# Head sums of squares by PE transposes and DVE row sums, and the mixers' large POOL operations on DVE and ACT

## The chip, the core and the metric

One core of one Trainium2 chip runs the whole program as one launch. The metric is device microseconds of one execution, median of three runs. The engines are called by the profile's names: PE (TensorE; its weight loads are the row PEld), DVE (VectorE), ACT (ScalarE), POOL (GpSimd) and SP (which here only issues DMAs). Each works through its own instructions in a fixed order, and waits on the others by semaphores.

## What is computed

One encoder layer over 1024 new prompt rows and 32 sample rows (T = 1056 token columns). The change touches the mixers between the two feed-forward parts:

```python
h = rms_norm(x, mix_norm)
sq, sk, sv, hq, hf, hi, hg = split(h @ w_in, ...)
sq = rms_norm(heads(sq, 8), sb_q_gain)             # per head of 64
sk = rms_norm(heads(sk, 8), sb_k_gain)
sb_o = rms_norm(sb_mix(sq, sk, sv), sb_out_gain)   # stick-breaking attention, per head of 64
f = lb + (1.0 - lb) * sigmoid(hf)
k_in = (1.0 - lb) * sigmoid(-hf)
q_h = silu(hq)
o_h, S_new = hgrn2_scan(q_h, k_in, hi, log(f), S0) # 4 heads of 128
o_h = rms_norm(o_h, hg_out_gain) * silu(hg)        # per head of 128
x = x + concat([sb_o, o_h]) @ w_out
```

All is float32. Each per-head `rms_norm` needs one sum of squares per token and head.

## The kernel before

Features lie on the 128 partitions and tokens on the free axis, in three groups of 384, 384 and 288 tokens (`GROUPS`). The program has a feed-forward part (to about 740 us), the mixers (about 740 to 1480 us) and a second feed-forward part. In the mixers `project_stream` multiplies 28 slabs of `w_in` (tile `pp`, L840, each product as three matmuls of split operands), and `mix_stream` those of `w_out` (`ps`, L1447). Between these, `merge` lays the steps of the attention streams (`z`, `pt`, `av`), the sample streams and the scans (`hg_stream`); a scheduler sets each engine's final order from that and from priorities. So the filler matmuls `pp` stand between the small steps of the streams, and the order does not change at run time.

Two things are touched.

**Sums of squares.** `token_factors` gets the squares `sq` (128 features by up to 384 tokens; two heads of 64 or one of 128 on the partitions). Each block of 128 tokens is a matmul (L222, tile `pmc`) with `sq` as the weights and a two-column or one-column matrix of 1/64 or 1/128 (`g.hd`, `g.od`) as the moving side. DVE reads the few sums from PSUM (L226 with a factor for the token, or L229 with the epsilon); POOL adds the epsilon (L227), raises to -1/2 (L230) and multiplies by the token's factor (L232). `spread` then widens the factors on ACT (L242, `wide`), PE transposes them (L249, `pb`), and DVE multiplies them in (L926, L933, L1054, L1415). It is called 52 times: 24 for q and k, 16 for the attention's output, 12 for the scans' output, in 140 blocks of 128 tokens and 4 of 32.

**Large elementwise work on POOL.** In `hg_jobs`: (1 - lb) and lb on `hk` and `hf` (L1276, L1278), and the products with a sigmoid for `hq` and `hg` (L1283). In `hg_stream`: seven levels of a doubling scheme per head. A level has PE products `pl` (L1347); then, on the 1024 prompt tokens, `hk` times `hf` on POOL (L1358), and `hq` times `hf` (L1360), a predicated copy of `pl` into `att` (L1362) and an update of `hf` (L1363) on DVE. The next level's `pl` reads `hk` and `hq`. At the end stands the gate (L1417). In `sb_jobs`: the low part of the split values `V` (L974; the high part is a cast on DVE, L973).

The PSUM tiles `pmc`, `pb`, `pl` and others share three buffers (tag `px`).

Of the kernel before, what the change touches and what calls it, by code (L numbers as in the profile page):

```python
# [24 lines left out]
TG = 384  # L25
# [34 lines left out]
def more_consts(g, pool, w):  # L60
# [152 lines left out]
def token_factors(g, f, psp, sq, w, means, behind_, tokens=None):  # L213


    nc = g.nc
    nb, rows, nh = -(-w // P), min(w, P), means.shape[1]
    mc = psp.tile([P, 512], F32, name="pmc", tag="px", bufs=3)
    v = f[0:rows, 0:nb, 0:nh]
    with behind(g, behind_):  # L220
        for b in range(nb):
            nc.tensor.matmul(mc[0:rows, b * nh:(b + 1) * nh], sq[:, b * P:b * P + rows], means, start=True, stop=True)  # L222
    src = mc[0:rows, 0:nb * nh].rearrange("p (b h) -> p b h", h=nh)
    wide = lambda t: t[:, :, None].broadcast_to([rows, nb, nh])
    if tokens is not None:
        nc.vector.tensor_tensor(out=v, in0=src, in1=wide(g.r2[0:rows, tokens]), op=ALU.mult)  # L226
        nc.gpsimd.tensor_scalar(out=v, in0=v, scalar1=1.0, scalar2=EPS, op0=ALU.mult, op1=ALU.add)  # L227
    else:
        nc.vector.tensor_scalar(out=v, in0=src, scalar1=EPS, scalar2=None, op0=ALU.add)  # L229
    nc.gpsimd.tensor_tensor(out=v, in0=v, in1=g.mh[0:rows, :, None].broadcast_to([rows, nb, nh]), op=ALU.pow)  # L230
    if tokens is not None:
        nc.gpsimd.tensor_tensor(out=v, in0=v, in1=wide(g.rc[0:rows, tokens]), op=ALU.mult)  # L232
# [633 lines left out]
def sb_jobs(g, m, pool, psp, gi, outs):  # L866
# [30 lines left out]
    def qk(nm, gain):  # L897
        def evacuate(n, ps):
# [15 lines left out]
            def factors():  # L914
                with g.tc.high_priority():
                    token_factors(g, f[:, b0:b0 + 3], psp, sq, TG, g.hd, g.filler, slice(b0, b0 + 3))
                    if nm == "qn":
                        nb = min(3, 8 - b0)
                        nc.gpsimd.tensor_scalar(out=t.minus[:, b0:b0 + nb], in0=f[:, b0:b0 + nb], scalar1=-1.0,
                                                scalar2=0.0, op0=ALU.mult, op1=ALU.add)  # L920
                        return sample_q if n == NG - 1 else None
                return normed
# [44 lines left out]
    def rows(n):  # L967
# [5 lines left out]
        nc.vector.tensor_copy(hi, src)  # L973
        nc.gpsimd.tensor_tensor(out=lo, in0=src, in1=hi, op=ALU.subtract)  # L974
# [66 lines left out]
def sb_out_norm(g, pool, psp, o, w, out):  # L1041
# [3 lines left out]
    def factors(c):  # L1045
# [4 lines left out]
        token_factors(g, f[c], psp, sq, cw, g.hd, g.filler)  # L1050
# [198 lines left out]
def hg_jobs(g, m, pool, psp, hh):  # L1249
# [5 lines left out]
    def evac(nm):  # L1255
        def evacuate(n, ps):
# [12 lines left out]
            if nm == "hf":  # L1269

                if n == 0:
# [4 lines left out]
                nc.gpsimd.tensor_scalar(out=kd, in0=kd, scalar1=g.olb[:, hh:hh + 1], scalar2=0.0,  # L1276
                                        op0=ALU.mult, op1=ALU.add)
                nc.gpsimd.tensor_scalar(out=xd, in0=xd, scalar1=g.olb[:, hh:hh + 1], scalar2=g.lb[:, hh:hh + 1],  # L1278
                                        op0=ALU.mult, op1=ALU.add)
            else:  # L1280
                a = pool.tile([P, TG], F32, name="sp", tag="sq", bufs=2)[:, 0:gw(n)]
                nc.scalar.activation(a, xd, AF.Sigmoid)
                nc.gpsimd.tensor_tensor(out=xd, in0=xd, in1=a, op=ALU.mult)  # L1283
# [25 lines left out]
def hg_stream(g, m, pool, psp, hh, state, outs, out):  # L1309
# [28 lines left out]
    while m_ < P:  # L1338

        for b, (b0, nch, L) in enumerate(blocks):  # L1340
# [16 lines left out]
            eng = nc.gpsimd if b == 0 else nc.vector  # L1357
            eng.tensor_tensor(out=kv[:, :, 0, :], in0=kv[:, :, 0, :], in1=tr.broadcast_to([P, nb2, m_]),  # L1358
# [45 lines left out]
    def factors(n):  # L1404
# [6 lines left out]
        token_factors(g, fo[n], psp, sq, TG, g.od, g.filler)  # L1411

    def normed(n):
# [3 lines left out]
        nc.gpsimd.tensor_tensor(out=o[:, gs(n)], in0=o[:, gs(n)], in1=sg[:, gs(n)], op=ALU.mult)  # L1417
# [460 lines left out]
```

## Time and profile before

| | us |
|---|---|
| median of 3 runs (2212.99 to 2214.30) | 2213.72 |
| the profiled execution | 2215.67 |
| its span, first to last instruction | 2214.0 |
| PE busy | 2152.4 (97%) |
| DVE, ACT, POOL busy | 1437.6, 928.3, 721.8 |
| PE, DVE, POOL busy in 740 to 1480 us | 720.0, 465.9, 233.5 |
| mean granted TensorE clock | 0.988 |

Busy time of PE includes the modelled ends of pipelined matmuls, so it says where PE had work, not that it ran at its peak. A float32 product is two records (two loads, two matmuls); a transpose of a float32 block, and a product of split operands, is one. "Idle before" in a row is time in which that engine had nothing to run, with what ended it.

### The profile page before, as it was taken

The page shows a single profiled execution, that of the slowest core. Times are in us where ns is not written, and L with a number is a line of the kernel's source. Part 1 is how long each engine was busy: PE and PEld are TensorE (multiplying, and loading weights), DVE is VectorE, ACT ScalarE, POOL GpSimd, SP SyncE. Part 2 cuts the span into 40 slices and gives each one's busy share as a digit, 9 for nine tenths or more (in the row PEclk, how much of TensorE's full clock was granted, in tenths as well). Part 3 has the DMA queues.
Part 4 walks back from the last instruction along what each step waited for, and adds up shares of the span by engine and source line. Part 5 has one row for each costly group of instructions (what it writes and reads, how often), then busy time and mean ns, then how long its engine had stood idle before and what let it go on. Part 6 is the DMA issues. An engine that isn't in the chain of part 4 may idle for free.

```text
span 2214.0 us, 41837 instructions
## 1 busy us (share of the span) xinstructions
PE 2152.4 (97%) x16475; PEld 2102.7 (95%) x16475; DVE 1437.6 (65%) x2461; ACT 928.3 (42%) x1812; POOL 721.8 (33%) x957
## 2 busy tenths in 40 slices
PE   8999999999999999999999999998999999999998
PEld 7999999999999999999999998898999999999998
DVE  5876666654668457567567578449766666645675
ACT  6423333323447444454544555236322333334443
POOL 1455544440004322333333333122555543420000
PEclk9999999999999998999999999999999999999999
DMA  8575454448534210120120122383676455467343
GB/s 239 177 214 170 140 183 153 151 130 295 180 128 153 91 55 20 43 69 20 43 69 20 46 80 79 122 251 124 210 221 193 139 179 162 143 218 243 126 150 122
DMA packets 328806, 307.30 MB, mean 139 GB/s; under 512 B 26593, under 2 KB 284897, under 8 KB 328609
## 3 DMA queue, kind: packets, MB, share of 16 engines
q1 hardware_dynamic: 259456, 264.75, 37.0%
q10 hardware_dynamic: 68672, 38.25, 6.0%
q8 instruction: 129, 2.11, 0.4%
q0 software_dynamic: 480, 1.62, 0.2%
q14 instruction: 69, 0.56, 0.1%
HBM read 208.46 MB, written 96.11 MB: 138 GB/s over the span
## 4 chain that ended last, share of the span: by engine, by line
PE 52%; DVE 5%; DMA 4%; POOL 2%; issue 2%; ACT 1%; SPq 0%; DVEq 0%; ACTq 0%; POOLq 0%
PE bk L389 15%; PE pp L840 14%; PE bk L704 10%; PE pl L1347 2%; PE ps L1447 2%; PE av L1116 1%; PE pt L1097 1%; PE pmc L222 1%; PE z L1152 1%; PE z L1151 1%; DVE t L1010 1%; PE ps L1468 1%; PE pb L249 1%; DMA xp<-xd 1%; DMA gt<-pd 0%
## 5 line engine op out<-in xcount | busy, mean ns | idle before, releaser
L704 PE MATMUL bk<-tl,wh 128*128 128x256 f32 x1232 | 351.3, 285 | 4.6 <-DVE tl L662 4.5
L704 PE MATMUL bk<-th,wl 128*128 128x256 f32 x1232 | 350.1, 285 | 0.4 <-DVE wl L651 0.4
L704 PE MATMUL bk<-th,wh 128*128 128x256 f32 x1232 | 348.8, 284 | 0.9 <-ACT th L661 0.8
L840 PE MATMUL pp<-xs_a,wh 128*128 128x384 f32 (+1 forms) x1008 | 263.8, 343 | 0.0
L704 PEld LDWEIGHTS bk<-tl,wh 128*128 128x128 f32 x1232 | 232.7, 189 | 6.4 <-DVE tl L662 6.4
L704 PEld LDWEIGHTS bk<-th,wl 128*128 128x128 f32 x1232 | 232.5, 189 | 0.9 <-DVE wl L651 0.7
L704 PEld LDWEIGHTS bk<-th,wh 128*128 128x128 f32 x1232 | 231.6, 189 | 1.6 <-ACT th L661 1.3
L544 POOL TENSOR_TENSOR gt<-gt,b 128x256 f32<-128x256 f32 x88 | 73.8, 839 | 328.0 <-ACT gt L543 319.4
L840 PEld LDWEIGHTS pp<-xs_a,wh 128*128 128x128 f32 x1008 | 171.0, 191 | 6.0 <-issue 4.1
L651 DVE SCALAR_TENSOR_TENSOR wl<-oraw,wh 128x1024 fp32r<-128x1024 f32 x84 | 97.9, 1166 | 104.9 <-ACT wh L650 104.8
L840 PE MATMUL pp<-xs_a,wl 128*128 128x384 f32 (+1 forms) x504 | 165.5, 328 | 0.0
L650 ACT ACTIVATE wh<-oraw 128x1024 fp32r<-128x1024 f32 x84 | 83.7, 997 | 147.3 <-PE bk L704 127.7
L389 PE MATMUL bk<-ops_a,wh 128*128 128x272 f32 (+1 forms) x704 | 132.9, 289 | 2.0 <-ACT e L370 2.0
L163 ACT ACTIVATE wh<-wraw 128x512 fp32r<-128x512 f32 (+2 forms) x122 | 89.2, 747 | 106.5 <-PE pp L840 37.2
L543 ACT ACTIVATE gt<-gt 128x256 f32<-128x256 f32 x88 | 37.3, 424 | 224.2 <-DVE gt L510 224.1
L164 DVE TENSOR_TENSOR wl<-wraw,wh 128x512 fp32r<-128x512 f32 (+2 forms) x122 | 110.3, 918 | 29.9 <-ACT wh L163 29.1
L548 POOL TENSOR_TENSOR gt<-gt,b 128x256 f32<-128x256 f32 x88 | 89.1, 1013 | 80.3 <-DVE b L510 80.3
L389 PEld LDWEIGHTS bk<-ops_a,wh 128*128 128x128 f32 x704 | 111.2, 192 | 2.6 <-ACT e L370 2.5
L389 PE MATMUL bk<-ops_a,wl 128*128 128x272 f32 (+1 forms) x352 | 101.1, 288 | 2.6 <-DVE wl L164 2.6
L1514 POOL TENSOR_TENSOR rstd<-rstd,nsq 128x512 f32<-128x512 f32 (+1 forms) x28 | 33.8, 1233 | 205.2 <-ACT nsq L1513 205.2
L1008 ACT ACTIVATE t<-z,minus 128x128 f32<-128x128 f32 (+2 forms) x96 | 55.6, 580 | 98.8 <-PE z L1154 75.4
L840 PEld LDWEIGHTS pp<-xs_a,wl 128*128 128x128 f32 x504 | 96.3, 191 | 0.0
(467 smaller groups left out, 6980.0 us busy)
## 6 DMA issues: line engine op xcount, KB each, us to landing
wraw<-in_ffn_w_in_dram SPq DMA_DIRECT2D x58, 512.0 KB, 4.3
oraw<-in_ffn_w_out_dram SPq DMA_DIRECT2D x94, 256.0 KB, 4.6
sd<-osum SPq DMA_DIRECT2D x44, 512.0 KB, 3.1
gd<-gt SPq DMA_DIRECT2D x42, 528.0 KB, 5.0
braw<-in_ffn_w_in_dram ACTq DMA_DIRECT2D x42, 512.0 KB, 4.3
oraw<-sd SPq DMA_DIRECT2D x40, 512.0 KB, 3.7
oraw<-in_ffn_w_out_dram SPq DMA_DIRECT2D x30, 512.0 KB, 3.4
wraw<-in_w_in_dram SPq DMA_DIRECT2D x28, 512.0 KB, 3.7
```

What stands on the lines that cost most here:

```text
L163: nc.scalar.activation(hi, src, AF.Copy)
L164: return nc.vector.tensor_tensor(out=lo, in0=src, in1=hi, op=ALU.subtract)
L389: mm = g.nc.tensor.matmul(ps, wt[x][:, kk, :], xt[y][:, kk, :], start=(first and kk == 0 and n == 0), stop=(kk == HK - 1 and n == len(PASS ...
L544: nc.gpsimd.tensor_tensor(out=gt[:, 1, cc], in0=gt[:, 1, cc], in1=s["b2"], op=ALU.mult)
L548: last = nc.gpsimd.tensor_tensor(out=gt[:, 0, cc], in0=gt[:, 0, cc], in1=s["b1"], op=ALU.mult)
L650: nc.scalar.activation(h, r, AF.Copy, scale=0.5)
L651: nc.vector.scalar_tensor_tensor(out=l, in0=r, scalar=0.5, in1=h, op0=ALU.mult, op1=ALU.subtract)
L704: nc.tensor.matmul(ps, wt[a][:, d * P:(d + 1) * P], xt[b][:, cols(c)], start=(k == 0 and n == 0), stop=(k == FH - 1 and n == len(PASSES) - 1))
L840: g.filler = nc.tensor.matmul(ps[:, 0:gw(n)], wt[a][:, k, :], xs(b, k)[:, gs(n)], start=(k == 0 and j == 0), stop=(k == KC - 1 and j == le ...
L1008: nc.scalar.activation(a, z, AF.Sigmoid, scale=minus)
L1347: nc.tensor.matmul(pl[0:L, c, 0:hl].rearrange("p (b m) -> p b m", m=m_), k[:, cs(b, c)], qr, start=True, stop=True)
L1447: nc.tensor.matmul(ps[:, 0:w], wt[a][:, k, :], xs(b, c)[:, gs(n)], start=(k == 0 and i == 0), stop=(k == 5 and i == len(PASSES) - 1))
```

## The change

`token_factors` now transposes each block of `sq` (tokens to partitions) and lets DVE sum the rows from PSUM with one TENSOR_REDUCE over 64 or 128 elements. The token's factor and the mean with its epsilon go to POOL: one more small POOL operation in each of the 52 calls. `hd` and `od` go. The gate, the products with sigmoids, `hf`'s affine step and the levels' `hk` move from POOL to DVE, `hk`'s scaling to ACT, `V`'s high part from DVE to ACT and its low part from POOL to DVE.

```diff
@@ -61,13 +62,6 @@
     nc = g.nc
     g.identr = pool.tile([P, P], F32R, name="identr")
     nc.vector.tensor_copy(g.identr, g.ident)
-
-    g.hd = pool.tile([P, 2], F32, name="hd")
-    nc.gpsimd.memset(g.hd, 0.0)
-    nc.gpsimd.memset(g.hd[0:64, 0:1], 1.0 / 64)
-    nc.gpsimd.memset(g.hd[64:128, 1:2], 1.0 / 64)
-    g.od = pool.tile([P, 1], F32, name="od")
-    nc.gpsimd.memset(g.od, 1.0 / P)
     g.zero = pool.tile([P, 1], F32, name="zero")
     nc.gpsimd.memset(g.zero, 0.0)
 
@@ -210,23 +204,22 @@
 EXP_LN, SIGMOID = "natural_log_exp_and_others", "sigmoid_and_others"
 
 
-def token_factors(g, f, psp, sq, w, means, behind_, tokens=None):
-
-
-    nc = g.nc
-    nb, rows, nh = -(-w // P), min(w, P), means.shape[1]
-    mc = psp.tile([P, 512], F32, name="pmc", tag="px", bufs=3)
+def token_factors(g, f, psp, sq, w, behind_, tokens=None):
+
+
+    nc = g.nc
+    nb, rows, nh = -(-w // P), min(w, P), f.shape[2]
+    mc = psp.tile([P, 3, P], F32, name="pmc", tag="px", bufs=3)
     v = f[0:rows, 0:nb, 0:nh]
     with behind(g, behind_):
         for b in range(nb):
-            nc.tensor.matmul(mc[0:rows, b * nh:(b + 1) * nh], sq[:, b * P:b * P + rows], means, start=True, stop=True)
-    src = mc[0:rows, 0:nb * nh].rearrange("p (b h) -> p b h", h=nh)
+            nc.tensor.transpose(mc[0:rows, b, :], sq[:, b * P:b * P + rows], g.ident)
+    nc.vector.tensor_reduce(out=v.rearrange("p b h -> p (b h)"),
+                            in_=mc[0:rows, 0:nb, :].rearrange("p b (h d) -> p (b h) d", h=nh), axis=AX.X, op=ALU.add)
     wide = lambda t: t[:, :, None].broadcast_to([rows, nb, nh])
     if tokens is not None:
-        nc.vector.tensor_tensor(out=v, in0=src, in1=wide(g.r2[0:rows, tokens]), op=ALU.mult)
-        nc.gpsimd.tensor_scalar(out=v, in0=v, scalar1=1.0, scalar2=EPS, op0=ALU.mult, op1=ALU.add)
-    else:
-        nc.vector.tensor_scalar(out=v, in0=src, scalar1=EPS, scalar2=None, op0=ALU.add)
+        nc.gpsimd.tensor_tensor(out=v, in0=v, in1=wide(g.r2[0:rows, tokens]), op=ALU.mult)
+    nc.gpsimd.tensor_scalar(out=v, in0=v, scalar1=nh / P, scalar2=EPS, op0=ALU.mult, op1=ALU.add)
     nc.gpsimd.tensor_tensor(out=v, in0=v, in1=g.mh[0:rows, :, None].broadcast_to([rows, nb, nh]), op=ALU.pow)
     if tokens is not None:
         nc.gpsimd.tensor_tensor(out=v, in0=v, in1=wide(g.rc[0:rows, tokens]), op=ALU.mult)
@@ -913,7 +906,7 @@
 
             def factors():
                 with g.tc.high_priority():
-                    token_factors(g, f[:, b0:b0 + 3], psp, sq, TG, g.hd, g.filler, slice(b0, b0 + 3))
+                    token_factors(g, f[:, b0:b0 + 3], psp, sq, TG, g.filler, slice(b0, b0 + 3))
                     if nm == "qn":
                         nb = min(3, 8 - b0)
                         nc.gpsimd.tensor_scalar(out=t.minus[:, b0:b0 + nb], in0=f[:, b0:b0 + nb], scalar1=-1.0,
@@ -970,8 +963,8 @@
         o, b0, nb = natural(lambda c, e: t.vT[:, GROUPS[n][0] + c:GROUPS[n][0] + c + e], n, outs["v_p"], True)
         src = o[:, 0:nb, :].rearrange("p b (h d) -> p b h d", h=2)
         hi, lo = t.V[:, b0:b0 + nb, :, 0:64], t.V[:, b0:b0 + nb, :, 64:128]
-        nc.vector.tensor_copy(hi, src)
-        nc.gpsimd.tensor_tensor(out=lo, in0=src, in1=hi, op=ALU.subtract)
+        nc.scalar.activation(hi, src, AF.Copy)
+        nc.vector.tensor_tensor(out=lo, in0=src, in1=hi, op=ALU.subtract)
 
     return [(lambda: (gi < 1 or m.dup_done[gi - 1]) and (gi < 2 or m.sampled[gi - 2]), qk("kn", g.kg)),
             (lambda: True, qk("qn", g.qg)), (lambda: gi < 1 or m.sb[gi - 1].V is not None, v)]
@@ -1047,7 +1040,7 @@
         sq = g.wp.tile([P, TG], F32, name="sq", tag="xp", bufs=3)
         nc.scalar.activation(sq[:, 0:cw], o[:, c:c + cw], AF.Square)
         f[c] = pool.tile([P, 3, 2], F32, name="fo", tag="fo", bufs=3)
-        token_factors(g, f[c], psp, sq, cw, g.hd, g.filler)
+        token_factors(g, f[c], psp, sq, cw, g.filler)
 
     def normed(c):
         cw = min(TG, w - c)
@@ -1273,14 +1266,13 @@
                 kd = t.k[:, gs(n)]
                 nc.scalar.activation(kd, xd, AF.Sigmoid, scale=-1.0)
                 nc.scalar.activation(xd, xd, AF.Sigmoid)
-                nc.gpsimd.tensor_scalar(out=kd, in0=kd, scalar1=g.olb[:, hh:hh + 1], scalar2=0.0,
-                                        op0=ALU.mult, op1=ALU.add)
-                nc.gpsimd.tensor_scalar(out=xd, in0=xd, scalar1=g.olb[:, hh:hh + 1], scalar2=g.lb[:, hh:hh + 1],
+                nc.scalar.activation(kd, kd, AF.Copy, scale=g.olb[:, hh:hh + 1])
+                nc.vector.tensor_scalar(out=xd, in0=xd, scalar1=g.olb[:, hh:hh + 1], scalar2=g.lb[:, hh:hh + 1],
                                         op0=ALU.mult, op1=ALU.add)
             else:
                 a = pool.tile([P, TG], F32, name="sp", tag="sq", bufs=2)[:, 0:gw(n)]
                 nc.scalar.activation(a, xd, AF.Sigmoid)
-                nc.gpsimd.tensor_tensor(out=xd, in0=xd, in1=a, op=ALU.mult)
+                nc.vector.tensor_tensor(out=xd, in0=xd, in1=a, op=ALU.mult)
             if nm == "hg" and n == NG - 1:
                 return [lambda: lambda: setattr(t, "ready", True)]
             return []
@@ -1354,8 +1346,7 @@
             qv, kv, fv = (x[:, b0 * P:b0 * P + W].rearrange("p (b two m) -> p b two m", two=2, m=m_)
                           for x in (q, k, f))
             tl, tr = fv[:, :, 0, m_ - 1:m_], fv[:, :, 1, m_ - 1:m_]
-            eng = nc.gpsimd if b == 0 else nc.vector
-            eng.tensor_tensor(out=kv[:, :, 0, :], in0=kv[:, :, 0, :], in1=tr.broadcast_to([P, nb2, m_]),
+            nc.vector.tensor_tensor(out=kv[:, :, 0, :], in0=kv[:, :, 0, :], in1=tr.broadcast_to([P, nb2, m_]),
                               op=ALU.mult)
             nc.vector.tensor_tensor(out=qv[:, :, 1, :], in0=qv[:, :, 1, :], in1=tl.broadcast_to([P, nb2, m_]),
                                     op=ALU.mult)
@@ -1408,13 +1399,13 @@
         if w < TG:
             nc.gpsimd.memset(sq[:, w:TG], 0.0)
         fo[n] = pool.tile([P, 3, 1], F32, name="fh", tag="fh", bufs=3)
-        token_factors(g, fo[n], psp, sq, TG, g.od, g.filler)
+        token_factors(g, fo[n], psp, sq, TG, g.filler)
 
     def normed(n):
         w = gw(n)
         nc.vector.scalar_tensor_tensor(out=o[:, gs(n)], in0=o[:, gs(n)], scalar=g.hgo[:, 0:1],
                                        in1=spread(g, psp, fo[n], 0, w), op0=ALU.mult, op1=ALU.mult)
-        nc.gpsimd.tensor_tensor(out=o[:, gs(n)], in0=o[:, gs(n)], in1=sg[:, gs(n)], op=ALU.mult)
+        nc.vector.tensor_tensor(out=o[:, gs(n)], in0=o[:, gs(n)], in1=sg[:, gs(n)], op=ALU.mult)
         out(*GROUPS[n], o[:, gs(n)])
 
     yield from skewed(factors, normed, range(NG))
```

The feed-forward parts keep their order. On PE, between the first two levels of the first scan head, the rows before were (`av` is the attention's, `pp` the filler; the last row is the second level):

```order
L1116 MATMUL av<-sbl,V 128x128
L840 MATMUL pp<-xs_a,wh 128x288 x2
L840 MATMUL pp<-xs_a,wl 128x288
L840 MATMUL pp<-xs_b,wh 128x288 x2
L840 MATMUL pp<-xs_b,wl 128x288
L840 MATMUL pp<-xs_a,wh 128x288 x2
L840 MATMUL pp<-xs_a,wl 128x288
L840 MATMUL pp<-xs_a,wh 128x288
L1347 MATMUL pl<-hq,hk 128x64 x8
```

Now, at the same place:

```order
L1109 MATMUL av<-sbl,V 128x128
L833 MATMUL pp<-xs_a,wh 128x288 x2
L833 MATMUL pp<-xs_a,wl 128x288
L833 MATMUL pp<-xs_b,wh 128x288 x2
L833 MATMUL pp<-xs_b,wl 128x288
L833 MATMUL pp<-xs_a,wh 128x288 x2
L833 MATMUL pp<-xs_a,wl 128x288
L833 MATMUL pp<-xs_a,wh 128x288 x2
L833 MATMUL pp<-xs_a,wl 128x288
L833 MATMUL pp<-xs_a,wh 128x288 x2
L833 MATMUL pp<-xs_a,wl 128x288
L1339 MATMUL pl<-hq,hk 128x64 x8
```

Three more rows of filler stand ahead of the second level's products. On DVE, from the attention step ahead of it (`t`) to the update of `hf`, before:

```order
L1010 SCALAR_TENSOR_TENSOR t_10853<-t_10852,left,zero 128x512
L1012 TENSOR_TENSOR t_10852<-z,t_10853 128x512
L1360 TENSOR_TENSOR hq<-hq,hf 128x512
L1362 COPY_PREDICATED att<-lmask_3107,pl 128x512
L1363 TENSOR_TENSOR hf<-hf 128x512
```

and now:

```order
L1003 SCALAR_TENSOR_TENSOR t_10854<-t_10853,left,zero 128x512
L1005 TENSOR_TENSOR t_10853<-z,t_10854 128x512
L1349 TENSOR_TENSOR hk<-hk,hf 128x512
L1351 TENSOR_TENSOR hq<-hq,hf 128x512
L1353 COPY_PREDICATED att<-lmask_3101,pl 128x512
L1354 TENSOR_TENSOR hf<-hf 128x512
```

The 512-element `hk`, which was on POOL beside these, stands ahead of `hq`. On POOL, the factors of the first k and q groups before (`sq` is the padding of later squares):

```order
L227 TENSOR_SCALAR fkn<-fkn 128x6
L230 TENSOR_TENSOR fkn<-fkn,mh 128x6
L232 TENSOR_TENSOR fkn<-fkn,rc 128x6
L912 MEMSET sq 128x96
L227 TENSOR_SCALAR fqn<-fqn 128x6
L230 TENSOR_TENSOR fqn<-fqn,mh 128x6
L232 TENSOR_TENSOR fqn<-fqn,rc 128x6
L919 TENSOR_SCALAR minus<-fqn 128x6
```

and now:

```order
L221 TENSOR_TENSOR fkn<-fkn,r_2523 128x6
L222 TENSOR_SCALAR fkn<-fkn 128x6
L223 TENSOR_TENSOR fkn<-fkn,mh 128x6
L225 TENSOR_TENSOR fkn<-fkn,rc 128x6
L905 MEMSET sq 128x96
L221 TENSOR_TENSOR fqn<-fqn,r_2523 128x6
L222 TENSOR_SCALAR fqn<-fqn 128x6
L223 TENSOR_TENSOR fqn<-fqn,mh 128x6
L225 TENSOR_TENSOR fqn<-fqn,rc 128x6
L912 TENSOR_SCALAR minus<-fqn 128x6
```

Each chain has one operation more, the token's factor, which was on DVE in L226.

## Rows read from the trace of the kernel before

**Rows 1.** The page: busy us (share) of each engine; the chain's shares by engine.

```profile
PE 2152.4 (97%) x16475; PEld 2102.7 (95%) x16475; DVE 1437.6 (65%) x2461; ACT 928.3 (42%) x1812; POOL 721.8 (33%) x957
...
PE 52%; DVE 5%; DMA 4%; POOL 2%; issue 2%; ACT 1%; SPq 0%; DVEq 0%; ACTq 0%; POOLq 0%
```

**Rows 2.** Stretches: window us, length, each engine's busy us (count), clock, DMA share, GB/s.

```profile
740.00:1480.00 740.00, 720.03 (x4930) 678.97 (x4929) 465.87 (x893) 350.49 (x764) 233.45 (x404) 0.98 0.23 68
```

**Rows 3.** Chain of waits, 740 to 1480 us, shares of that stretch by line.

```profile
by line: PE pp L840 41.0%; PE pl L1347 6.1%; PE ps L1447 4.8%; PE av L1116 4.1%; PE pt L1097 3.5%; PE pmc L222 3.2%; PE z L1152 2.2%; PE z L1151 2.1%; DVE t L1010 2.0%; issue 1.7%; PE pb L249 1.6%; DMA xp<-xd 1.5%; PE pu L1387 1.3%; DMA xd<
```

**Rows 4.** Groups, PEld, 740 to 1480 us: operands, count, busy us, mean ns, idle.

```profile
L222 PEld LDWEIGHTS pmc<-hd,sq 128*128 128x128 f32 x208 | 28.5, 198 | 4.4 <-DVE sbl L164 3.0 <-ACT KT L1197 0.9
...
L222 PEld LDWEIGHTS pmc<-od,sq 128*128 128x128 f32 x72 | 9.3, 191 | 0.0
L249 PEld LDWEIGHTS pb<-ident,wide 128*128 128x128 f32 x64 | 9.0, 160 | 5.8 <-ACT wide L242 3.7 <-DVE wl L164 1.6
```

**Rows 5.** PEld in order of time at 943 us: start, us, line, operands, count.

```profile
943.05 0.42 PEld L249 LDWEIGHTS pb<-ident,wide 128*128 128x128 f32 x3
943.44 0.75 PEld L222 LDWEIGHTS pmc<-od,sq 128*128 128x128 f32 x6
944.11 0.30 PEld L840 LDWEIGHTS pp<-xs_a,wh 128*128 128x128 f32 x2
```

**Rows 6.** Groups, PE, 740 to 1480 us, columns as in rows 4.

```profile
L1347 PE MATMUL pl<-hq,hk 128*128 128x64 f32 x448 | 57.9, 285 | 6.6 <-DVE att L1362 4.9 <-DVE sbl L164 0.8 <-POOL hk L1358 0.5
...
L1097 PE MATMUL pt<-ident,t 128*128 128x128 f32 x288 | 48.3, 277 | 0.6 <-DVE sbl L164 0.5 <-DVE att L1332 0.2
```

**Rows 7.** PE's idle time ahead of pb (L249): released by, us, times.

```profile
  ACT wide L242: 7.0, 7
  POOL fh L230: 3.8, 5
```

**Rows 8.** Groups, DVE, 740 to 1480 us, columns as in rows 4.

```profile
L1360 DVE TENSOR_TENSOR hq<-hq,hf 128x512 f32<-128x512 f32 x28 | 23.6, 841 | 29.3 <-PE pl L1347 29.3
...
L1010 DVE TENSOR_TENSOR_SCAN t<-t,zero 128x384 f32<-128x384 f32 x16 | 15.3, 956 | 2.8 <-ACT t L1008 2.7
...
L863 DVE TENSOR_TENSOR ko<-pn,rc 128x384 f32<-128x384 f32 x8 | 4.5, 558 | 10.1 <-PE pn L879 10.0 <-PE z L1154 0.2
...
L973 DVE CAST V<-ko 128x384 fp32r<-128x384 f32 x8 | 2.9, 360 | 0.3
...
L226 DVE TENSOR_TENSOR fkn<-pmc,r 128x6 f32<-128x6 f32 x12 | 1.9, 162 | 10.6 <-PE pmc L222 10.6
...
L1390 DVE COPY S<-pu 128x128 f32<-128x128 f32 x4 | 1.1, 285 | 0.9 <-PE pu L1387 0.9
```

**Rows 9.** Groups, POOL, 740 to 1480 us, columns as in rows 4.

```profile
L1358 POOL TENSOR_TENSOR hk<-hk,hf 128x512 f32<-128x512 f32 x28 | 44.4, 1585 | 62.0 <-PE pl L1347 61.8
...
L1283 POOL TENSOR_TENSOR hq<-hq,sp 128x384 f32<-128x384 f32 x8 | 8.1, 1014 | 15.6 <-ACT sp L1282 15.6
...
L227 POOL TENSOR_SCALAR fqn<-fqn 128x6 f32<-128x6 f32 x12 | 3.2, 266 | 35.8 <-DVE fqn L226 35.8
```

**Rows 10.** In order of time, between two levels of the first scan head.

```profile
868.14 1.53 POOL L1358 TENSOR_TENSOR hk<-hk,hf 128x512 f32<-128x512 f32 x1 [3.78 <-PE pl L1347]
...
868.37 1.85 DVE L1360 TENSOR_TENSOR hq<-hq,hf 128x512 f32<-128x512 f32 x1
...
870.14 1.28 DVE L1362 COPY_PREDICATED att<-lmask,pl 128x512 f32<-128x512 uint8 x1
...
871.56 0.30 PE L1347 MATMUL pl<-hq,hk 128*128 128x64 f32 x1 [1.64 <-DVE att L1362]
```

**Rows 11.** Stretches of 10 us, columns as in rows 2.

```profile
870.00:880.00 10.00, 8.44 (x40) 8.10 (x41) 5.98 (x14) 1.90 (x4) 2.49 (x3) 0.63 0.00 0
880.00:890.00 10.00, 10.00 (x43) 9.75 (x43) 5.05 (x16) 1.89 (x4) 4.15 (x5) 0.52 0.00 0
...
1350.00:1360.00 10.00, 9.28 (x63) 8.06 (x62) 9.94 (x14) 9.09 (x16) 3.33 (x6) 1.00 0.38 129
```

More of the change, by code (lines that the diff above doesn't have):

```diff
@@ L13 @@
 ALU = mybir.AluOpType
+AX = mybir.AxisListType
 PSUM = bass.MemoryType.PSUM
```

## The prediction

> **What bounds the kernel now.** I read the page first. PE is busy for 97% of the span and carries 52% of the chain that ended last, with DVE at 5% and POOL at 2% [rows 1]. The reader should see that a microsecond of PE work is worth most, and that work on other engines costs only where PE waits for it. The change lies in the mixers alone, so I read that stretch next: in 740 us PE has work for 720.0, the weight loads for 679.0, DVE for 465.9 (63%), ACT for 350.5 and POOL for 233.5 [rows 2]. PE's own idle time is thus 20 us. The chain in that stretch is again mostly PE, and `pmc`, the small products that the change replaces, has 3.2% of it: 740 x 0.032 = 23.7 us [rows 3]. Then I read the groups by shape, for prices, and two places in order of time.
>
> The profiled execution took 2215.67 us around a span of 2214.0; the median of the runs is 2213.72. I add the terms to the median, since the two differ by less than 0.1%. What a measurement of this kernel can tell from no change is about 0.2%, 4.4 us: below 2209.3 is faster, above 2218.1 slower.
>
> **1. Sums of squares on PE.** A block's product is two records, and the weights are the squares themselves, so PE spends its time loading 128 columns twice in order to stream one or two. In order of time, three such blocks (six loads) start at 943.44 and the next load starts at 944.11: 0.67 us. Directly ahead, three transposes of the very shape that replaces them start at 943.05 and give way at 943.44: 0.39 us [rows 5]. That is 0.223 against 0.130 us a block, 0.093 less. There are 140 full blocks (24 + 12 + 8 calls of three, 4 of two): 13.1 us of PE time go; the four blocks of 32 tokens I price at nothing. In all `pmc` now takes 140 x 0.223 = 31.2 us, near its two groups' 28.5 + 9.3 us of overlapping loads [rows 4]. Of this 23.7 us are on the chain, 76%, so the term is 13.1 x 0.76 = **-9.9 us**, between 0 (something else ends just as late each time) and -13.1.
>
> A single transposing matmul is shown as 277 ns long in its group [rows 6], about twice the pace of rows 5, because the next one starts before it ends. The Trainium skill (TensorE: Matmul & The Clock Gate, Part 4: PE-mode transpose) gives about 275 ns for a transpose in a kernel's context, which agrees as a duration. If it were the pace, three blocks would take 0.83 us instead of 0.67, and the term would be +5.7 us (140 x 0.053 x 0.76); the pace in rows 5 decides against that.
>
> **2. The levels of the scans.** At the first level of a head POOL's `hk` starts at 868.14 and takes 1.53 us; DVE's `hq`, two inputs from SBUF like it, starts 0.23 us later and takes 1.85 us, against a group mean of 841 ns. Then `att` takes 1.28 us, and PE, with its filler used up, idles 1.64 us until `att` is done [rows 8, 10]. PE's group has three such waits, 4.9 us together [rows 6]. Now `hk` and `hq` are one behind the other on DVE. Twenty-eight `hq` sum to 23.6 us; if four of them are the 1.85 us kind, the other 24 take 0.67 us each, and I take 0.67 us for both operations when POOL is not beside them. From 868.37 `hk`, `hq` and `att` would end at 868.37 + 0.67 + 0.67 + 1.28 = 870.99, near 0.4 us earlier than now, and the new order has 15 matmuls of filler there in place of 10, about 0.7 us more. So the 1.64 us shrink to about 0.5: -3.4 us for three heads. In later levels the next `pl` waited for POOL's 1.6 us where it now waits for 1.34 us of DVE; with 24 of those, mostly covered by filler, I take -1. The term is **-4.4 us**, between -8 and 0; zero if DVE is late with the attention's scan ahead of `hk`, on which both kernels depend alike.
>
> **3. More work on DVE.** The row sum is an operation that the trace does not show. Its nearest rows are the one-input copy from PSUM, 285 ns for 128 elements, and the two-input operation from PSUM, 558 ns for 384; the most it could be is the scan's 956 ns for 384 [rows 8]. I take 0.56 us for 384, since the first two lie on a line of 1.07 ns an element ((558 - 285) / 256): 44 of these, 4 of 256 at 0.4 and 4 of 128 at 0.29 make 27.4 us, less 52 small operations at 0.16 (162 ns in the group): +19.1. The rest, by 0.56 us for 384 and 0.45 for 288 elements: 28 `hk` at 0.67 less four times the 1.18 us by which `hq` was stretched, +14.0; 24 products with a sigmoid, +12.6; 12 gates, +6.3; 12 affine steps at 0.36 (the cast's 360 ns), +4.3; `V` loses 12 casts and gains 12 subtractions, +2. The sum is 58 us, and DVE in the mixers goes from 63% to 71%.
>
> What lands on the path: DVE's 5% of the chain is 111 us of its 1437.6 busy [rows 1], 7.7%, and 58 x 0.077 = **+4.5 us**. The lower bound is nothing, the upper a quarter, +14.5, because DVE is full in places (9.94 of 10 us at 1350 [rows 11]). New waits are in this term: where `hq` is scaled and multiplied with only ACT's sigmoid between, DVE now stands still for that half microsecond, with the attention's scan queued behind it; POOL stood there before for up to 15.6 us in eight [rows 9], and nobody minded.
>
> **4. The longer chain to `pb`.** From `pmc` to the widened factors DVE takes 0.56 in place of 0.16, and POOL has one more small operation, 0.27 us at the group's mean: +0.67 us. PE idled 7.0 + 3.8 us ahead of `pb`, in 12 of its places [rows 7]. If all 12 grow by 0.67, +8; if the new order, which sets the first `pb` one filler matmul later, covers them, nothing. POOL, with 1585 ns operations gone from its queue [rows 9], also starts each chain sooner. I take **+2 us**.
>
> **5. What costs nothing.** POOL loses the 44.4 us of `hk` and 72 more operations of mostly 1 us [rows 9], some 113 us, which no longer delay the small copies for the attention's scans; DVE waits for these too rarely to count. ACT gains 12 scalings and 12 copies at about 0.5 us, 11 us in 740 where it is busy for 47%; `V` and `hk` are read many steps later, which is their cover, and without it each would cost its half microsecond. The two constants and the SP queue change nothing.
>
> Sum: -9.9 - 4.4 + 4.5 + 2 = -7.8; 2213.7 - 7.8 = **2205.9 us**. Its own range, with each term at a moderate end, is 2200 to 2211.
>
> **The rivals.**
>
> - *The clock comes back too: 2197.* Just behind that 1.64 us wait the granted clock falls: 0.63 and 0.52 over 870 to 890 us [rows 11]. With levels of 1.2 and 2.4 GHz, that is 17 us at the lower one, up to 8.5 us lost. If the wait set it off, more filler and an earlier `att` take it away: -7.8 - 8.5. Against it: the wait is not all that stands ahead of the fall, and the first level's products stay as they are. Chance 0.17.
> - *PE waits longer by what it saves: 2213.* The chains to `pb` cost their full +8, DVE +7, and the level waits stay half as they are: -9.9 - 2.2 + 8 + 7 = +2.9, or, with the smaller of these, -3. For it: PE has only 20 us of idle time but DVE's queue is in order, and the order was laid for another mix. Against it: filler stands at nearly every place. Chance 0.22.
> - *DVE becomes the bound: 2230.* The mechanism is one: 58 us are put on an engine that is already full around 1350 us, and PE's `pt` and `av` come late. If half of it lands on the path, +29 - 9.9 - 4.4 + 2 = +16.7. It breaks even where 21% lands and is slower from 29%. For it: rows 11; against: 37% of DVE's time is free, and DVE had 7.7% on the chain. Chance 0.11.
> - *Transposes are no cheaper: 2221.* By the pace of 277 ns the first term is +5.7: +5.7 - 4.4 + 4.5 + 2 = +7.8. The skill's Part 4, weighed above, would be the page for it. The rows speak against it. Chance 0.03.
>
> **How the numbers follow.** My forecast, 2205.9, has 0.47; I put 0.04 of this above 2209.3. Faster: 0.43 + 0.17 = 0.60. Within 0.2%: 0.04 + 0.22 = 0.26. Slower: 0.11 + 0.03 = 0.14. The range takes in the forecast, the rival of waits, and most of the clock's: 2194 to 2219 leaves about 0.05 below and 0.13 above.
>
> **What will show it.** In the changed kernel's trace `pmc` should be 144 transposes, three at a pace near 0.39 us, and its share of the mixers' chain about 2%. The row sums should take about 0.56 us for 384 elements, DVE in the mixers about 524 us, POOL about 130. The wait of the second level's `pl` should be under 1 us in each head, and `hq` at the first level near 0.67 us. PE's idle time ahead of `pb` should be 11 to 15 us. I am wrong if DVE's share of the chain goes beyond 9%, if the mixers end no earlier though `pmc` costs less, or if the row sum is near 1 us, which alone adds 18 us of DVE work. A different granted clock between 860 and 900 us would show the first rival.

## The result, and the profile after

The changed kernel takes 2185.76 us (median of 4 runs, 2183.27 to 2187.86) against 2214.01 us of the kernel before beside it: a ratio of 0.9873, 95% interval 0.9854 to 0.9891, so 28 us faster. The forecast was 8 us, with 2194 as the low end of its range: the sign is right, the size is not.

First the page of the changed kernel, its engines and the chain's shares by engine [rows 1]; then one stretch of the mixers [rows 2] and the chain's shares there [rows 3].

```profile
PE 2123.6 (97%) x16331; PEld 2073.3 (95%) x16331; DVE 1476.6 (68%) x2537; ACT 937.5 (43%) x1836; POOL 631.9 (29%) x905
PE 54%; DVE 4%; DMA 3%; POOL 2%; ACT 1%; issue 1%; SPq 0%; ACTq 0%; DVEq 0%; POOLq 0%
```

```profile
740.00:1450.00 710.00, 690.21 (x4766) 647.80 (x4766) 504.85 (x962) 357.73 (x782) 142.19 (x353) 1.00 0.23 70
```

```profile
by line: PE pp L833 41.8%; PE pl L1339 6.4%; PE av L1109 4.5%; PE ps L1438 4.1%; PE pt L1090 4.0%; DMA xd<-xp 2.6%; PE z L1145 2.3%; PE z L1144 2.2%; DVE t L1003 1.9%; DMA xp<-xd 1.6%; PE pb L242 1.5%; PE pmc L216 1.5%; issue 1.4%; PE po L1
```

DVE has 39 us more work, but less of the chain (4% for 5%). `pmc` has 1.5% of 710 us, 10.7 us where it had 23.7. And the granted clock, the third number from the right, is 1.00 in the mixers, where it was 0.98.

In order of time, at the place of [rows 10] (the first head, first level to second), the changed kernel shows:

```profile
864.91 0.68 DVE L1349 TENSOR_TENSOR hk<-hk,hf 128x512 f32<-128x512 f32 x1
865.51 0.69 DVE L1351 TENSOR_TENSOR hq<-hq,hf 128x512 f32<-128x512 f32 x1
866.12 1.30 DVE L1353 COPY_PREDICATED att<-lmask,pl 128x512 f32<-128x512 uint8 x1
...
867.57 2.13 PE L1339 MATMUL pl<-hq,hk 128*128 128x64 f32 x18 [0.44 <-DVE att L1353]
```

`hk` and `hq` together take less than the stretched `hq` of 1.85 us did alone, and PE waits 0.44 us for 1.64. What hangs on it stands in the stretches behind it, before and after. Of before, the three at a lower clock that [rows 11] don't have (one, at 1039.8 us, begins in the stretch ahead of the first of these):

```profile
1040.00:1050.00 10.00, 9.88 (x61) 9.17 (x60) 6.76 (x14) 3.80 (x8) 6.53 (x7) 0.84 0.01 2
...
1200.00:1210.00 10.00, 10.00 (x58) 9.54 (x57) 5.92 (x17) 1.90 (x4) 4.33 (x4) 0.66 0.01 2
...
1260.00:1270.00 10.00, 10.00 (x61) 7.72 (x60) 2.75 (x7) 4.30 (x13) 3.20 (x4) 0.83 0.07 20
```

The first two stand right behind the waits of 1.63 us at the second and third head. The last does not: PE has no wait over 0.2 us in the 12 us ahead of it. After, at the first head:

```profile
870.00:880.00 10.00, 10.00 (x75) 9.37 (x74) 9.45 (x23) 4.71 (x10) 4.14 (x6) 1.00 0.00 0
880.00:890.00 10.00, 9.99 (x75) 9.38 (x75) 8.41 (x23) 4.71 (x9) 2.38 (x5) 1.00 0.16 48
```

PE is "busy" for 10 us of 880 to 890 in both kernels, but with 75 matmuls here and 43 there: at half the clock it does less, and its busy share hides that. The matmul count and the clock column show it.

For all kernels of this study I cut the profiled execution in the same way. The *projections* run from the first to the last start of `pp` (740.9 to 1350.4 us before, 738.3 to 1319.9 after), with three of the four scan heads in them. *Lost* is the sum, over the 10-us stretches from 740 to 1340 us, of 10 us x (1 - granted clock); *rest* is the projections less that; *tail* runs from the last `pp` to the end of the span. Each line is one execution.

| kernel | ratio to before (95%) | projections | lost | rest | tail |
|---|---|---|---|---|---|
| before | | 609.5 | 15.3 | 594.2 | 863.6 |
| changed | 0.9873 (0.9854 to 0.9891) | 581.6 | 0 | 581.6 | 861.6 |
| changed, again | 0.9867 (0.9852 to 0.9882) | 581.5 | 0 | 581.5 | 861.7 |
| e1 sums only | 0.9954 (0.9933 to 0.9975) | 597.7 | 6.9 | 590.8 | 869.7 |
| e2 moves only | 0.9910 (0.9888 to 0.9931) | 588.7 | 1.7 | 587.0 | 867.2 |
| e3 `hk` only | 0.9912 (0.9886 to 0.9937) | 589.7 | 0 | 589.7 | 862.9 |
| e4 `hk` back | 0.9933 (0.9911 to 0.9955) | 594.7 | 5.1 | 589.6 | 867.7 |
| e5 `hk`, first level | 0.9948 (0.9928 to 0.9967) | 593.0 | 3.4 | 589.6 | 866.1 |
| e6 `hk`, other levels | 0.9958 (0.9946 to 0.9971) | 598.0 | 5.1 | 592.9 | 865.8 |
| e7 wait back | 0.9905 (0.9887 to 0.9922) | 587.6 | 1.7 | 585.9 | 863.4 |
| e8 short chain | 0.9901 (0.9887 to 0.9916) | 579.8 | 0 | 579.8 | 872.5 |
| e10 out products | 0.9887 (0.9868 to 0.9906) | 580.7 | 0 | 580.7 | 869.9 |
| e11 wait doubled | 0.9932 (0.9912 to 0.9953) | 590.1 | 5.1 | 585.0 | 869.7 |
| e12 mixed chain | 0.9895 (0.9878 to 0.9912) | 582.9 | 3.4 | 579.5 | 870.4 |

The two profiled executions are 32.4 us apart. 27.9 of these lie in the projections, and 15.3 of the 27.9 answer to the lower clock that is gone; 2.6 lie ahead of them and 2.0 behind.

The lower clock is not the luck of one execution. The record has the mean granted clock of each, which gives what it cost over the whole span, span x (1 - clock): 25.0 us as the mean of 37 executions of the kernel before (18 to 33), 11.2 as that of the changed kernel's eight (9 to 15). These executions differ by 30 us in the mean, so some 14 of the 30 are the clock's.

### The profile page after: what moved, and what is told of

Read it like the earlier page. It is cut to its first block, busy times and chain, and to the rows that moved or that the text cites. A ratio compares the mean times of both kernels' runs of the same rounds, so it can differ in the third digit from the quotient of the medians.

```text
span 2181.5 us, 41553 instructions
## 1 busy us (share of the span) xinstructions
PE 2123.6 (97%) x16331; PEld 2073.3 (95%) x16331; DVE 1476.6 (68%) x2537; ACT 937.5 (43%) x1836; POOL 631.9 (29%) x905
## 4 chain that ended last, share of the span: by engine, by line
PE 54%; DVE 4%; DMA 3%; POOL 2%; ACT 1%; issue 1%; SPq 0%; ACTq 0%; DVEq 0%; POOLq 0%
PE bk L382 17%; PE pp L833 14%; PE bk L697 10%; PE pl L1339 2%; PE av L1109 1%; PE ps L1438 1%; PE pt L1090 1%; DMA xd<-xp 1%; PE ps L1459 1%; PE z L1145 1%; PE z L1144 1%; DVE t L1003 1%; DMA oraw<-in_ffn_w_out_dram 1%; DMA xp<-xd 1%; PE pb L242 1%
## 5 line engine op out<-in xcount | busy, mean ns | idle before, releaser
L833 PE MATMUL pp<-xs_a,wh 128*128 128x384 f32 (+1 forms) x1008 | 258.2, 338 | 0.0
L503 DVE TENSOR_TENSOR gt<-bk,p 128x256 f32<-128x256 f32 (+1 forms) x60 | 25.9, 432 | 109.7 <-PE bk L382 107.8
```

The source lines that it names most:

```text
L833: g.filler = nc.tensor.matmul(ps[:, 0:gw(n)], wt[a][:, k, :], xs(b, k)[:, gs(n)], start=(k == 0 and j == 0), stop=(k == KC - 1 and j == le ...
```

## The experiments

**Which part of the change?** Theory W: the long wait ahead of the second level, which `hk` on POOL beside `hq` on DVE makes, sets off the lower clock. Rival T: the transposes keep the clock up. The change splits into the new `token_factors` (e1) and everything else (e2); of that, `hk` alone is e3, and e4 takes it out of the changed kernel.

```diff
 # e1: before, with this part alone; e2: the changed kernel without it
-            nc.tensor.matmul(mc[0:rows, b * nh:(b + 1) * nh], sq[:, b * P:b * P + rows], means, start=True, stop=True)
+            nc.tensor.transpose(mc[0:rows, b, :], sq[:, b * P:b * P + rows], g.ident)
...
 # e3: before, with this part alone; e4: the changed kernel without it
-            eng = nc.gpsimd if b == 0 else nc.vector
-            eng.tensor_tensor(out=kv[:, :, 0, :], in0=kv[:, :, 0, :], in1=tr.broadcast_to([P, nb2, m_]),
+            nc.vector.tensor_tensor(out=kv[:, :, 0, :], in0=kv[:, :, 0, :], in1=tr.broadcast_to([P, nb2, m_]),
```

> The kernel before with the new sums of squares alone (transposes, row sums on DVE, one more small POOL operation per chain); every large POOL operation stays on POOL. Theory W (the wait at the second level of a scan head, made long by POOL's hk beside DVE's hq, is what the low clock follows): the waits of about 1.6 us and the stretches at the lower clock stay, some 30 us of them in 740 to 1440 us; PE work falls by 13 us, PE waits longer ahead of pb by about 9; time 2204 to 2212. Rival T (the transposes themselves keep the clock up, since they replace products that stream two columns): no stretch of the mixers below full clock, time near 2195, and hq at the first level still 1.8 us.

> The changed kernel with the old sums of squares (two-column products, sums read by DVE as before); all moves from POOL to DVE and ACT kept. Theory W: hq at the first level 0.69 us, the second level's wait under 0.6 us, no low clock in the scans; 15 us from the clock and about 5 from the waits are gained, time 2192 to 2198, pmc again near 3% of the mixers' chain. Rival T: the low clock stays as before the change, time 2206 to 2212.

> The kernel before with one edit: the levels' hk on DVE in place of POOL. Theory W: as the run with all moves, since the other moved operations are nobody's wait: 2193 to 2200, hq 0.69 us at the first level, clock 1.00 in the scans of the first three heads. Rival T, or a rival by which POOL's other large operations matter (they hold back the small POOL operations of the attention): 2207 to 2213.

> The changed kernel with one edit undone: the levels' hk back on POOL. Theory W: the 1.8 us hq, the waits of 1.6 us at the second levels and the low clock are back, time 2200 to 2207, some 18 us over the changed kernel. Rival T: the clock stays full, only the waits come back, time 2188 to 2192.

Measured: 2207.96, 2196.99, 2197.62 and 2203.01 us, beside 2216.98 of the kernel before. The times lie in W's ranges in all four, in T's in none. The one moved product, `hk`, is worth 19 us; the new sums 9; and all other moves from POOL, with 15 us of DVE work (507 against 492 from 730 to 1480 us), nothing that can be told from zero (e2 is 0.6 us faster than e3). That the gain on `hk` is the clock's for the greater part is seen in the table: lost 0 in e3, with 4.5 us less in the rest.

What W said of the clock holds only in part. With the new sums, the waits of 1.65 us stay in e1 (1.71 in e4), but 6.9 and 5.1 us are lost where the kernel before lost 15.3; e1 was to have some 30 us at the lower clock and has 14. Over all executions e1 lost 19.0 us as a mean against 27.1 of the kernel before beside it, which is nearly its whole gain. So the sums bear on the clock too: the runs refute T as the whole cause, not as a part of it. The trace of before shows how that may be. The fall at 1265 us, the one without a wait, begins right behind the products that the transposes replace, which stream two columns or one:

```profile
1262.73 0.81 PE L222 MATMUL pmc<-hd,sq 128*128 128x2 f32 x6
...
1264.28 0.72 PE L222 MATMUL pmc<-od,sq 128*128 128x1 f32 x6
```

These two groups follow each other closely once in each of the first three heads. In the seven kernels that keep them for the outputs, five of the 21 places have a fall that begins within 0.7 us behind (before 1265 us, e2 1087, e5 1092, e12 1083 and 1240), none of them with a wait of PE over 0.2 us in the 12 us ahead. With transposes at these places, in seven executions, none of 21 has one. This was counted afterwards; no run tests it.

**Is it the first level?** At the first level of three heads POOL starts first; at the second `hq` is 0.04 us ahead and takes 0.69 us, and POOL's product is the one that takes longer. (One later `hq` is stretched too, to 1.44 us, at the sixth level of the third head.) Of before, DVE and POOL at the second level:

```profile
874.38 0.69 DVE L1360 TENSOR_TENSOR hq<-hq,hf 128x512 f32<-128x512 f32 x1 [1.46 <-PE pl L1347]
874.42 2.01 POOL L1358 TENSOR_TENSOR hk<-hk,hf 128x512 f32<-128x512 f32 x1 [4.71 <-PE pl L1347]
```

e5 moves `hk` at the first level only, e6 at the six others.

```diff
-            eng = nc.gpsimd if b == 0 else nc.vector
+            eng = nc.gpsimd if b == 0 and m_ > 1 else nc.vector    # e5
+            eng = nc.gpsimd if b == 0 and m_ == 1 else nc.vector   # e6
```

> The kernel before, with the scan's hk product on VectorE at the first of the seven levels only; the other six stay on POOL. In the trace of before it is only there that hk starts ahead of hq (868.14 against 868.37 us) and that hq takes 1.85 us, not 0.69. Theory W (that stretched product, the 1.6 us for which PE then waits ahead of the second level, and the lower clock behind it are what the whole move of hk takes away): as good as all seven levels, 2195 to 2202 us. Rival S (each of the seven levels gives its part): about a seventh of the 19 us, 2207 to 2214 us.

> The complement: the kernel before, with hk on VectorE at the second to the seventh level and on POOL at the first. Theory W: hq stays at 1.85 us at each head's first level, PE's wait of 1.6 us ahead of the second stays, and nearly nothing is won, 2208 to 2216 us. Rival S: six sevenths of the 19 us, 2195 to 2202 us.

Measured: 2202.3 and 2206.17 us, beside 2215.74. Neither theory holds as it was put: by the ratios the first level is worth 11.5 us and the six others 9.3. The first level weighs as much as all the rest, but it is not all. In e6, which keeps `hk` on POOL at the first level alone, PE's wait and the clock behind it are plain; its first head in order of time, and its stretches at the three heads:

```profile
866.47 1.53 POOL L1358 TENSOR_TENSOR hk<-hk,hf 128x512 f32<-128x512 f32 x1 [3.78 <-PE pl L1347]
...
866.70 1.85 DVE L1360 TENSOR_TENSOR hq<-hq,hf 128x512 f32<-128x512 f32 x1
...
869.89 2.19 PE L1347 MATMUL pl<-hq,hk 128*128 128x64 f32 x18 [1.64 <-DVE att L1362]
```

```profile
870.00:880.00 10.00, 9.90 (x64) 9.19 (x65) 6.66 (x19) 3.50 (x8) 1.91 (x4) 0.83 0.00 0
...
1030.00:1040.00 10.00, 9.91 (x64) 9.16 (x65) 6.62 (x19) 3.46 (x8) 1.91 (x4) 0.83 0.01 2
...
1190.00:1200.00 10.00, 9.46 (x61) 8.83 (x61) 6.84 (x19) 2.92 (x7) 1.91 (x4) 0.83 0.01 2
```

Three heads, three falls, each right behind the wait: 0.83 is 3.4 us at the lower level, 1.7 us lost. In the kernel before the same wait was followed by 0.63 and 0.52 [rows 11]: the fall is longer where the later levels have POOL's product too, which fits e6's share, though no run shows that by itself.

**The wait, or the contention?** e7 puts the wait back into the changed kernel without POOL, by a second copy on DVE that writes the same values again; e11 by two.

```diff
             nc.vector.copy_predicated(dst, msk, src)
+            if b == 0 and m_ == 1:
+                nc.vector.copy_predicated(dst, msk, src)   # e11: twice
```

> The changed kernel, with the copy of the first level's products into att issued twice (the second writes the same values): 1.3 us more of VectorE at each of the four heads' first level, with no product on POOL. It puts back PE's wait ahead of the second level without the contention of POOL and VectorE. Theory W (the wait itself, and a lower clock that it sets off, were the cost): four waits of 1.3 us more, 5 us, and 5 to 12 us of lower clock behind some of them: 2194 to 2204 us. Rival C (the contention, not the wait): 5 us at most, 2187 to 2192 us, and no stretch of lower clock.

> The changed kernel, with the copy of the first level's products into att issued three times: 2.6 us more of VectorE at each head's first level (one repeat was 1.3 us and 7.7 us of time). Theory W (a wait of PE of 2 us or more at a thin place is followed by a stretch of lower clock): 10 us of delay and a stretch of 0.83 or lower behind most of the four: 2197 to 2208 us. Rival C (the delay alone): 2192 to 2196 us, with no stretch of lower clock behind the first levels.

Measured: 2193.77 us beside 2186.12 of the changed kernel (7.7 more), between the two ranges, and 2201.56 us, in W's. In e7 PE's wait ahead of the second level is 0.95 us, the delay in the projections 4.3 us by the rest, and the clock falls behind the wait in one of the three heads. In e11 the wait is 1.41 us, and the clock falls in two of the three:

```profile
871.11 2.20 PE L1339 MATMUL pl<-hq,hk 128*128 128x64 f32 x18 [1.41 <-DVE hf L1357]
```

```profile
870.00:880.00 10.00, 8.35 (x52) 7.86 (x53) 7.82 (x17) 1.35 (x4) 2.16 (x6) 0.83 0.00 0
...
1030.00:1040.00 10.00, 10.00 (x54) 9.55 (x53) 6.62 (x15) 1.78 (x5) 2.02 (x5) 0.66 0.01 2
```

With no product on POOL, a longer wait brings the lower clock back (the scheduler also put a few more filler matmuls ahead of it). So the wait sets it off, and the contention mattered because it made the wait. It is not certain behind each wait. At the first head, e1 has the wait of e6 and almost the same order of PE around it, and full clock behind it:

```profile
868.28 2.14 PE L1340 MATMUL pl<-hq,hk 128*128 128x64 f32 x18 [1.65 <-DVE att L1355]
...
870.00:880.00 10.00, 9.04 (x64) 8.05 (x63) 7.71 (x16) 3.77 (x8) 6.67 (x8) 1.00 0.01 2
```

Counted over all profiled executions, three heads each, a fall begins within 2.4 us of the second level's start in 9 of 12 heads with a wait of 1.63 to 1.71 us (before, e1, e4, e6), 2 of 3 with 1.41, 1 of 3 with 0.95, and 0 of 24 with 0.42 to 0.77.

**The longer chain to `pb`.** In the changed kernel PE's idle time ahead of `pb` (its line with the weight loads) is released by:

```profile
  ACT wide L235: 20.0, 18
  POOL fh L223: 2.6, 4
```

That is 22.6 us for 10.8 [rows 7]. But this view counts a wait twice, once before the weight load and once before the matmul behind it. The matmuls alone, before and then after (us, times, the longest):

```profile
PE pb L249 <- ACT wide L242: 2.8, 2, 1.6
...
PE pb L249 <- DVE so L1054: 0.8, 1, 0.8
...
PE pb L249 <- POOL fh L230: 0.7, 1, 0.7
...
PE pb L249 <- DVE hf L1415: 0.5, 1, 0.5
```

```profile
PE pb L242 <- ACT wide L235: 8.7, 8, 1.8
...
PE pb L242 <- POOL fh L223: 0.9, 1, 0.9
...
PE pb L242 <- DVE so L1047: 0.3, 1, 0.3
```

So PE stands still for 9.9 us ahead of `pb` where it did for 4.8. e8 makes the chain shorter than before; e10 gives the outputs' factors (`fo`, `fh`) their products back; e12 is e10 with e8's chain for keys and queries.

```diff
 # e8 (r2 now holds eps / (rc * rc); the product with rc goes too; the branch for the outputs is left out here)
-        nc.gpsimd.tensor_tensor(out=v, in0=v, in1=wide(g.r2[0:rows, tokens]), op=ALU.mult)
-    nc.gpsimd.tensor_scalar(out=v, in0=v, scalar1=nh / P, scalar2=EPS, op0=ALU.mult, op1=ALU.add)
+        nc.vector.scalar_tensor_tensor(out=v, in0=v, scalar=nh / P, in1=wide(g.r2[0:rows, tokens]),
+                                       op0=ALU.mult, op1=ALU.add)
...
 # e10 (out_factors is token_factors of before)
-        token_factors(g, f[c], psp, sq, cw, g.filler)
+        out_factors(g, f[c], psp, sq, cw, g.hd, g.filler)
```

> The changed kernel with a shorter chain from the row sums to the spread factors: with rc*(rc*rc*m+eps)^-0.5 = (m+eps/(rc*rc))^-0.5 the table r2 holds eps/(rc*rc), VectorE scales and adds in one small operation behind the row sum, and POOL keeps the power alone (one operation for four). Theory P (the longer chain to the factors cost PE 9 to 12 us of waits ahead of pb): most of that comes back, 2175 to 2181 us. Rival H (PE is busy with other work there, or waits for the spreading copy on ScalarE whatever stands ahead of it): 2183 to 2188 us.

> The changed kernel, with the products by a column of ones kept for the factors of the outputs (fo, fh) and the transposes with row sums for those of the keys and queries (fkn, fqn). In the changed kernel PE waits 6.3 us ahead of pb in the outputs' norms, in the kernel before 2.0 us. Theory Q (the longer chain there is what PE waits for): those waits come back by some 4 us and PE's work grows by some 5 us: 2184 to 2189 us. Rival H (PE waits there because it arrives earlier): the waits stay or move, 2189 to 2194 us.

> As the run with products for the outputs, and the shorter chain for the keys and queries (eps/(rc*rc) in the table, VectorE scales and adds, POOL does the power alone). The two waits of 1.7 us ahead of the first keys' pb get shorter by 0.5 us each: 2182 to 2188 us, if no new stretch of lower clock comes with it; with one, as with the shorter chain everywhere, 2190 to 2194 us.

> The changed kernel itself, beside these two: 2183 to 2189 us.

Measured: 2192.7, 2192.22, 2193.94 and 2186.12 us. e8 missed both ranges: a kernel with less to do is 6.6 us slower than the changed one. Its projections are 1.8 us shorter; its tail is 11 us longer. PE in order of time at the same place of the fourth head, in e8 and then in the changed kernel:

```profile
1347.61 0.55 PE L242 MATMUL pb<-ident,wide 128*128 128x128 f32 x3 [0.88 <-ACT wide L235]
1349.28 1.09 PE L1189 MATMUL ptc<-ident,craw 128*128 128x128 f32 x4 [1.12 <-issue]
```

```profile
1348.77 0.55 PE L242 MATMUL pb<-ident,wide 128*128 128x128 f32 x3 [0.65 <-ACT wide L235]
1349.08 0.59 PE L1438 MATMUL ps<-xs_a,wh 128*128 128x384 f32 x2
```

The scheduler laid out another order for e8: the eleven `ps` matmuls that follow this `pb` in the changed kernel stand behind `ptc`, `pmc` and a level of `pl`. PE's order in e8:

```
L242 MATMUL pb<-ident,wide 128x128 x3
L1189 MATMUL ptc<-ident,craw 128x128 x4
L216 MATMUL pmc<-ident,sq 128x128 x2
L1339 MATMUL pl<-hq,hk 128x64 x8
L1339 MATMUL pl<-hq,hk 32x16
L1438 MATMUL ps<-xs_a,wh 128x384 x2
```

PE stands still twice in two microseconds, the second time for nothing that the profile shows ("issue"), and the stretch of e8 there is

```profile
1350.00:1360.00 10.00, 9.74 (x44) 8.99 (x43) 4.77 (x14) 2.35 (x5) 1.01 (x1) 0.54 0.21 65
```

So e8 does not settle what POOL's operations cost: its order is another one. Of the waits, PE's idle matmul time ahead of `pb` only went from 9.9 to 8.6 us. e10 says where they come from: with the outputs' products back it is 3.6 us, 3.4 of it at the first two groups of keys. So the waits in the outputs' norms hang on the new sums, as theory Q has it (which step of the longer chain makes them was not tested), and its projections are 0.9 us shorter; but the time is in rival H's range, since its tail is 8 us longer, with 0.86 at 1350 us and 0.66 at 1470. At 1350 e10 shows no wait just ahead (twelve of the products of two columns stand in the 6 us before), so there too a wait is not the only thing that brings the clock down. e12 lies in the range that it had for new stretches of lower clock, and has them (0.83 at 1080, 1240 and 1350 us). None of the three beats the changed kernel; by their ratios only e8, measured beside it, is clear of it.

## Why the prediction was right in sign and wrong in size

- **The clock: the step that failed.** The forecast gave it no term, and the rival that had it got a chance of 0.17. The rival's place and cause were read rightly as far as they go: against it stood that the wait is not all that is ahead of the fall, and e6, e7 and e11 show that a wait can set it off. But it was priced by the first head alone (8.5 us): the other two heads' waits add 5.1, and the fall behind the small products, which nobody had looked for, 1.7, which makes 15.3 (some 14 over all executions). Forecast and clock make 2213.7 - 7.8 - 15.3 = 2190.6, within 5 us of the result.
- **1, the sums.** The chain's share went down by 13.0 us (23.7 to 10.7), the upper bound of the term and not 76% of it. The transposes' pace was read rightly, and that of 277 ns is excluded: 144 loads keep PEld busy for 17.6 us (row below), where 280 took 37.8 [rows 4]. e1 alone is worth 9 us, near the term, but for another reason than the one given: in its profile 3.4 us in the rest and 8.4 at the clock, against 6.1 more in the tail, most of that lower clock too.
- **2, the levels.** -4.4, and e3's rest is 4.5 us shorter; PE's waits for `att` went from 4.9 to 1.3 us, `hq` takes 0.69 us at the first level. Right.
- **3, DVE.** No part of the +4.5 is seen. DVE grew by 39 us, not 58, and its share of the chain fell. A row sum of 384 elements takes 0.55 to 0.56 us (rows below), as estimated. What the moves other than `hk` add lies beside PE's work: e2 is as fast as e3. A share of DVE's time on the chain, 7.7%, is no price for work put elsewhere on DVE.
- **4, `pb`.** +2 was low, but inside its bounds: PE's idle time grew by 5.1 us (4.8 to 9.9). [rows 7] were misread, since their 12 waits are those of loads and matmuls together; PE's matmuls had five. Five of the nine that are not tiny now stand in the outputs' norms for ACT's copy, where the trace of before had none of that sort: the term let the old places grow and did not look for new ones. By the view of rows 7, the sign "11 to 15 us" came out at 22.6.

The changed kernel's groups of loads for the sums on PEld and of row sums on DVE (columns as in rows 4 and 8):

```profile
L216 PEld LDWEIGHTS pmc<-ident,sq 128*128 128x128 f32 x144 | 17.6, 140 | 2.9 <-issue 0.7 <-ACT wh L157 0.6 <-DVE fh L217 0.6
...
L217 DVE TENSOR_REDUCE fqn<-pmc 128x6 f32<-128x384 f32 x12 | 6.7, 557 | 4.1 <-PE pmc L216 4.0
L217 DVE TENSOR_REDUCE fkn<-pmc 128x6 f32<-128x384 f32 x12 | 6.6, 547 | 7.0 <-PE pmc L216 7.0
```

With what was measured in their place, the terms without the clock make -13.0 - 4.5 + 0 + 5.1 = -12.4, where the forecast had -7.8. That is near the -12.6 by which the changed kernel's rest is shorter; it is a rough check, since the first and the last are read over all of the mixers and the rest over the projections. By the runs, the rest's parts are -3.4 for the sums (e1) and -7.2 for the moves (e2), together -10.6. The last 2 us, and what decides whether the clock falls behind a given wait or a group of small products, stay open. Where each fall stands was seen in one execution of each kernel, two of the changed one.

## What to carry to other kernels

Where PE is the bound, read the granted clock in short stretches over the whole kernel, not only at the first wait that shows it, and price a wait with what follows: here three waits, 5 us in all, were followed by 13.6 us lost at the lower clock. Look also at what stands ahead of a fall that has no wait: here, in five places, it was products of two columns or one. A busy share of 10 in 10 does not show the lower clock; the count of matmuls does. And when an edit makes work cheaper in a kernel whose order a scheduler lays out, look at the order of the bounding engine: e8, with the shorter chain, is 6.6 us slower, and its clock falls at a thin place, one from which filler had moved away.

## What was not expected of the hardware

- Two operations of two inputs each, on DVE and POOL at once, don't share: the one that starts first runs as if alone and the other waits. With POOL first, `hk` ends at 869.67 and `hq`, begun at 868.37, at 870.22 [rows 10]; with DVE first, `hq` takes its 0.69 us and `hk` 2.01. The sixth level of the kernel before has the cleanest pair: `hk` takes 1.08 us whether `hq` begins 0.2 or 1.0 us behind it, and `hq` takes 1.44 us in the one case and 0.68 in the other. First the third head, then the first:

```profile
1227.86 1.08 POOL L1358 TENSOR_TENSOR hk<-hk,hf 128x512 f32<-128x512 f32 x1
1228.05 1.44 DVE L1360 TENSOR_TENSOR hq<-hq,hf 128x512 f32<-128x512 f32 x1
```

```profile
903.92 1.08 POOL L1358 TENSOR_TENSOR hk<-hk,hf 128x512 f32<-128x512 f32 x1
904.92 0.68 DVE L1360 TENSOR_TENSOR hq<-hq,hf 128x512 f32<-128x512 f32 x1
```

  Both on DVE take 1.3 us in all. The Trainium skill (SBUF — State Buffer, "Who interferes with whom") states that a DVE instruction with two SBUF inputs contends with a GpSimd instruction that reads SBUF, by an exclusive lock on a shared port pair, and that the order of issue decides which one is blocked; the trace agrees. The prediction read the 1.85 us and did not ask why only four of 28 `hq` are stretched (three to 1.85 us, one to 1.44).
- The small power on POOL, 128x6, is its longest step on the way to `pb`: 1.4 to 1.5 us as a mean, where the scaling ahead of it takes 0.24.
- The lower clock came behind waits of PE as short as 0.95 us (one of three heads), 1.41 (two of three), 1.63 to 1.71 (nine of twelve); in five other places it came right behind products of two columns or one, with no wait at all.
